# A depthwise convolution on TensorE, and sixteen output blocks under way during the modulation

## The chip, the cores and the metric

One core of one Trainium2 chip runs the whole kernel as one launch. The metric is the device time of that launch in microseconds. An execution of this kernel on the same chip repeats to some tenths of a per cent; three runs of the kernel before are given below.

The engines are named as the profile names them: PE is TensorE's matmul stream and PEld its weight loads, DVE is VectorE, ACT is ScalarE, POOL is GpSimd, SP is SyncE, whose queue issues all the DMAs here. PSUM is the memory that matmuls write, in eight banks of 128 x 512 float32; the rest is in SBUF or in HBM.

## The reference

The program is a two-layer decoder trunk on 256 tokens of 2048 channels, all float32. Layer 0 mixes tokens by a causal convolution module, layer 1 by stick-breaking attention; each is followed by a gated feed-forward part. Only the beginning, layer 0's mixer, is touched by the change:

```python
shift, scale, gate = ada_ln(c, mix_mod_w[0], mix_mod_b[0])      # silu(c) @ (2048 x 6144), + bias, in three parts
h = rms_norm(x, mix_norm_g[0]) * (1.0 + scale) + shift
u = h @ pw1_w + pw1_b                                           # 2048 x 4096, the "first product"
val, gt = jnp.split(u, 2, axis=-1)
u = val * jax.nn.sigmoid(gt)
u = causal_depthwise_conv(u, dw_w, dw_b)                        # 31 taps for each channel
u = jax.nn.silu(layer_norm(u, ln_g, ln_b))
x = x + gate * (u @ pw2_w + pw2_b)                              # 2048 x 2048, the "second product"
```

After it come layer 0's feed-forward part (whose shift and scale come from `ffn0`, a second modulation of the same shape), layer 1 and a last norm.

## The kernel before

Activations lie transposed, channels on the 128 partitions and the 256 tokens along the row: `xs[k]`, 16 tiles. A product keeps 128 x 128 blocks of weights in the array and moves 256 tokens past them. Weights come in **pieces** of eight blocks (512 KB, `raw`). Each piece is split into a high and a low part, `wh` by ScalarE (L213) and `wl` by VectorE (L214), and activations are split likewise (`hh`, `hl`; `zh`, `zl` for the second product). A block is then three matmuls (L251 `hh x wh`, L252 `hl x wh`, L253 `hh x wl`) into the block's PSUM bank.

**The modulation.** 128 columns of a modulation are one load of 1 MB (`mraw`) and one VectorE instruction that multiplies it by silu(c) and sums along the row (L276, `mod_reduce`); a small addition (L280) and, for the scale, L286 follow. Some parts go to TensorE instead: `mod_rows` multiplies silu(c) with 512 columns at a time, as float32 matmuls with 32 columns of weights in four column tiles of the array at once (L466), and turns the rows into columns with four small matmuls (L476) after ScalarE has copied the sums out of PSUM (L471). Before, the gate of `mix0`, the scale of `ffn0` and a part of the shift of `ffn0` are summed by TensorE.

**The head of the first product.** The contraction tiles of `h` become final one by one, as their scale and shift do (`start_tiles`): L276 twice, then `t` (L363, VectorE: x times scale times 1/rms), `hh` (L320) and `hl` (L321). Eight output blocks are under way at once, each in a bank of its own, so that each new tile has one piece of weights to meet. The other 24 blocks follow one after the other with all 16 tiles ready; the modulations to come run beside them as steps of a generator (`fill`, 0.6 steps a piece). Twelve of the later pieces are not split: they go to TensorE as float32 (L249, with `hf`, the sum of `hh` and `hl`, made by GpSimd, L506).

**The convolution.** When both halves of a channel tile are done, ScalarE takes the sigmoid (L524) and VectorE the product `u` (L528). `conv` then makes 31 taps of it: ScalarE multiplies 12 (L541), which GpSimd adds (L543, L545), VectorE does 18 as multiply-adds into a PSUM bank (L549), ScalarE the last one (L535), and L552 adds the two sums into `ys[j]`. It runs as a generator in `side`, beside the product.

**The layer norm and the second product.** Sums over channels are matmuls with a matrix of ones (L569), of 14 tiles first; from them comes a first mean, which VectorE subtracts (L580), ScalarE squares (L582) and TensorE sums (L583). Then come the deviation (L349, L351), two VectorE instructions and a Silu per tile (L622, L623, L624), the split (L317, L318), and the second product.

**What sets the order.** Each engine works through its instructions in a fixed order. The framework places them when the program is built, by priorities and by its own estimate of when each can run; semaphores make an engine wait. All loads stand in SP's queue in the order of the program (`load`), so a DMA that waits holds back those behind it. `raw` has six buffers, `mraw` three, the split weights four.

Of the kernel before, what the change touches and what calls it, by code (L numbers as in the profile page):

```python
# [17 lines left out]
PB = 8  # 128x128 blocks of weights in a piece  # L18
# [7 lines left out]
PRODUCTS = 8       # buffers between ScalarE and GpSimd  # L26
# [10 lines left out]
def plan(nbs, kts, first, stagger=4):  # L37
    """Order of the (output block, contraction tile) pairs of a product."""
# [9 lines left out]
class Cfg:  # L48
    def __init__(self, D, T, H, F, CW, FW):
# [3 lines left out]
        self.GH = 4  # L53
        self.rows0 = min(ROWS, KD // 4 - 1)

# [15 lines left out]
        items = [("c", KD), ("mix_g0", KD), ("mix_b0", 3 * KD), ("pw1_b", 2 * KD), ("cdw", KD * CW), ("cdb", KD), ("ln_g", KD), ("ln_b", KD),  # L71
# [6 lines left out]
        pl["pw1"] = plan(pairs, kd, min(8, 2 * KD), 0)  # L78
# [29 lines left out]
def hybrid_trunk(ctx: ExitStack, tc: tile.TileContext, cfg: Cfg, io: dict):  # L108
# [28 lines left out]
    # ---------------------------------------------------------------- constants and activations  # L137
# [53 lines left out]
    plain = {("pw1", i) for i in range(KD, 4 * KD) if i % PLAIN[0] == PLAIN[1]} if KD > 8 else set()  # L191
# [13 lines left out]
    def split_next():  # L205
        """High and low parts, of 12 significant bits each, of the next piece of weights."""
        blocks, v, n = raws[len(parts)]
        if stream[len(parts)] in plain:
            parts.append((blocks, v, None))
            return  # L210
# [6 lines left out]
    def pieces(name):  # L217
        """The pieces of a plan; loads and splits run ahead, over the ends of the plans."""
# [15 lines left out]
    def gemm(name, xh, xl, done, after=None, banks=(), x=None, width=None):  # L234
        """Weights stationary: psum[128 outputs, T] for each output block; done(block, psum)."""
        set_rate(name)
        left, ps, banks = {}, {}, list(banks)
        for nb, _ in cfg.plans[name]:
            left[nb] = left.get(nb, 0) + 1
        for blocks, wh, wl in pieces(name):  # L240
            for b, (nb, kt) in enumerate(blocks):
                first = nb not in ps
                if first:
                    ps[nb] = (banks.pop(0) if banks else psum_acc)()
# [3 lines left out]
                if wl is None:  # L248
                    nc.tensor.matmul(o, wh[:, c], x[kt], start=first, stop=left[nb] == 0)  # L249
                else:  # L250
                    nc.tensor.matmul(o, wh[:, c], xh[kt], start=first, stop=False)  # L251
                    nc.tensor.matmul(o, wh[:, c], xl[kt], start=False, stop=False)  # L252
                    nc.tensor.matmul(o, wl[:, c], xh[kt], start=False, stop=left[nb] == 0)  # L253
# [113 lines left out]
    class Entry:  # L367
# [585 lines left out]
```

## Time and profile before

| | us |
|---|---|
| three runs | 2379.94, 2383.69 (median), 2388.55 |
| span of the profiled execution | 2373.7 |
| median less that span | 10.0 |
| mean granted TensorE clock | 0.983 |
| sixteenth modulated tile `hh` starts | 134.8 |
| last matmul of the first product (L249) ends | 323.8 |
| first Silu of the layer norm (L624) | 356.5 |
| first matmul of the second product (L251 with `zh`) | 357.9 |

The profiled execution has no time of its own beside its span; the span runs from the first to the last instruction on the core. A row of the groups gives the line, engine, operation, output and input tiles, their shapes, the count, and then the busy time, the mean of one in ns and what the engine waited for just before. A row of the chain or of the timeline gives the start, the length, the engine, the tile and the line. In rows by stretch, a busy engine is followed by the number of its records in brackets.

### The profile page before, as it was taken

What the parts mean: (1) busy time and instruction counts of PE and PEld (TensorE: products, weight loads), DVE (VectorE), ACT (ScalarE), POOL (GpSimd) and SP (SyncE); (2) the same over time, 40 slices, a digit from 0 to 9 for tenths busy, and PEclk for the clock granted to TensorE, in tenths of its full rate; (3) what the DMA queues carried; (4) which work ended last, traced back from release to release, by engine and by line L of the source; (5) the groups of instructions that cost most, each with busy time, mean ns of one, the idle gap of its engine ahead of it and who ended that gap; (6) DMA issues with size and microseconds to landing.
All of it is one profiled execution on the core that took longest, in us unless ns stands there. A gap on an engine that the chain in (4) does not pass through costs nothing.

```text
span 2373.7 us, 45095 instructions
## 1 busy us (share of the span) xinstructions
PE 2280.7 (96%) x18228; PEld 2194.9 (92%) x18228; DVE 1814.1 (76%) x2470; ACT 1219.0 (51%) x1828; POOL 335.1 (14%) x357
## 2 busy tenths in 40 slices
PE   5689989999999999999999999999999999999997
PEld 4677859999999999999998999999999999999997
DVE  8978988898878788788887667789876555666644
ACT  3266667665553345555465544556555434555443
POOL 2368652300000000000121000121000000000011
PEclk8799999999999999999999999999999999999999
DMA  8987879677769877778866676676865555566663
GB/s 341 350 342 279 299 261 354 209 264 282 274 249 354 311 275 291 265 278 322 317 239 241 240 254 238 239 250 260 292 216 187 187 187 187 187 188 187 188 186 105
DMA packets 138308, 603.62 MB, mean 254 GB/s; under 512 B 15346, under 2 KB 15474, under 8 KB 113522
## 3 DMA queue, kind: packets, MB, share of 16 engines
q1 hardware_dynamic: 138098, 600.74, 71.5%
q8 instruction: 142, 2.33, 0.4%
q14 instruction: 68, 0.55, 0.1%
HBM read 598.58 MB, written 2.10 MB: 253 GB/s over the span
## 4 chain that ended last, share of the span: by engine, by line
PE 82%; DVE 10%; issue 2%; POOL 2%; DMA 2%; ACT 2%; DVEq 0%; SPq 0%; POOLq 0%; ACTq 0%
PE ps L252 25%; PE ps L251 25%; PE ps L253 25%; DVE mraw L276 3%; DVE wl L214 2%; POOL y L545 2%; DMA mraw<-in_mt_ffn 1%; PE ps L787 1%; PE ps L788 1%; PE ps L789 1%; PE ps L249 1%; DVE auxb L549 1%; PE auxa L466 1%; DVE t L363 0%; DVE hl L321 0%
## 5 line engine op out<-in xcount | busy, mean ns | idle before, releaser
L213 ACT CAST wh<-raw 128x1024 fp32r<-128x1024 f32 x740 | 773.8, 1048 | 884.9 <-PE ps L252 652.1
L214 DVE TENSOR_TENSOR wl<-raw,wh 128x1024 fp32r<-128x1024 f32 x740 | 910.2, 1234 | 379.0 <-ACT wh L213 372.0
L251 PE MATMUL ps<-hh,wh 128*128 128x256 f32 (+1 forms) x3696 | 1036.6, 284 | 49.2 <-ACT hh L320 48.1
L252 PE MATMUL ps<-hl,wh 128*128 128x256 f32 (+1 forms) x3696 | 1044.1, 283 | 4.0 <-DVE hl L318 2.0
L253 PE MATMUL ps<-hh,wl 128*128 128x256 f32 (+1 forms) x3696 | 1039.0, 281 | 6.3 <-DVE wl L214 6.3
L251 PEld LDWEIGHTS ps<-hh,wh 128*128 128x128 f32 x3696 | 694.2, 190 | 63.0 <-ACT hh L320 52.5
L252 PEld LDWEIGHTS ps<-hl,wh 128*128 128x128 f32 x3696 | 709.2, 192 | 9.3 <-issue 3.4
L253 PEld LDWEIGHTS ps<-hh,wl 128*128 128x128 f32 x3696 | 704.2, 191 | 11.5 <-DVE wl L214 7.3
L252 PE MATMUL ps<-gl,wh 128*128 128x256 f32 x1408 | 396.2, 281 | 0.0
L251 PE MATMUL ps<-gh,wh 128*128 128x256 f32 x1408 | 396.2, 281 | 0.0
L253 PE MATMUL ps<-gh,wl 128*128 128x256 f32 x1408 | 396.2, 281 | 0.0
L276 DVE CUSTOM_DVE_ANT_0 mraw<-mraw,csr 128x2048 f32<-128x2048 f32 x152 | 347.6, 2287 | 56.2 <-DMA mraw<-in_mt_ffn 34.8
L336 POOL TENSOR_TENSOR sumsq<-sumsq,t 128x256 f32<-128x256 f32 x56 | 70.2, 1254 | 1570.4 <-ACT t L332 1570.1
L252 PEld LDWEIGHTS ps<-gl,wh 128*128 128x128 f32 x1408 | 265.0, 188 | 0.0
L251 PEld LDWEIGHTS ps<-gh,wh 128*128 128x128 f32 x1408 | 265.0, 188 | 0.0
L253 PEld LDWEIGHTS ps<-gh,wl 128*128 128x128 f32 x1408 | 265.0, 188 | 0.0
L656 DVE SCALAR_TENSOR_TENSOR t<-ps,par,t 128x254 f32<-128x254 f32 x336 | 160.4, 479 | 4.1
L545 POOL TENSOR_TENSOR y<-y,prod 128x256 f32<-128x256 f32 x160 | 144.4, 911 | 12.9 <-ACT prod L541 3.0
L549 DVE SCALAR_TENSOR_TENSOR auxb<-u,cpar,auxb 128x256 f32<-128x256 f32 x288 | 118.8, 481 | 1.1 <-ACT auxb L535 0.9
L541 ACT ACTIVATE prod<-u,cpar 128x256 f32<-128x256 f32 x192 | 85.5, 500 | 40.3 <-DVE u L528 24.1
L653 ACT ACTIVATE t<-ps,par 128x256 f32<-128x256 f32 x168 | 93.9, 560 | 0.0
L332 ACT ACTIVATE t<-x 128x256 f32<-128x256 f32 x75 | 30.1, 414 | 85.9 <-DVE x L676 37.0
(174 smaller groups left out, 2107.9 us busy)
## 6 DMA issues: line engine op xcount, KB each, us to landing
raw<-in_w_down SPq DMA_DIRECT2D x176, 512.0 KB, 4.3
mraw<-in_mt_mix SPq DMA_DIRECT2D x80, 1024.0 KB, 7.3
mraw<-in_mt_ffn SPq DMA_DIRECT2D x72, 1024.0 KB, 6.7
raw<-in_w_pw SPq DMA_DIRECT2D x96, 512.0 KB, 6.2
raw<-in_w_up01b SPq DMA_DIRECT2D x84, 512.0 KB, 4.9
raw<-in_w_up11b SPq DMA_DIRECT2D x84, 512.0 KB, 3.5
raw<-in_w_up00b SPq DMA_DIRECT2D x80, 512.0 KB, 4.6
raw<-in_w_up10b SPq DMA_DIRECT2D x80, 512.0 KB, 3.6
```

Of the source, the lines that this page charges most:

```text
L213: nc.scalar.copy(wh[:, :n], v[:, :n])
L214: nc.vector.tensor_tensor(wl[:, :n], v[:, :n], wh[:, :n].bitcast(F32), op=ALU.subtract)
L251: nc.tensor.matmul(o, wh[:, c], xh[kt], start=first, stop=False)
L252: nc.tensor.matmul(o, wh[:, c], xl[kt], start=False, stop=False)
L253: nc.tensor.matmul(o, wl[:, c], xh[kt], start=False, stop=left[nb] == 0)
L276: nc.vector.tensor_tensor_reduce(out=v, in0=v, in1=csr, scale=1.0, scalar=0.0, op0=ALU.mult, op1=ALU.add, accum_out=macc[:, nb:nb + 1])
L336: engine.tensor_tensor(self.sum, self.sum, sq, op=ALU.add)
L541: nc.scalar.activation(pr, u[:, i:i + T], AF.Copy, scale=tap(i))
L545: nc.gpsimd.tensor_tensor(y, y, pr, op=ALU.add)
L549: nc.vector.scalar_tensor_tensor(o, u[:, k:k + T], tap(k), o, op0=ALU.mult, op1=ALU.add)
L653: nc.scalar.activation(y, ps[:, :T], AF.Identity, bias=pc(f"fdb{i}", nb, 1), scale=w(FW - 1))
L656: nc.vector.scalar_tensor_tensor(y[:, s:], ps[:, :T - s], w(k), y[:, s:], op0=ALU.mult, op1=ALU.add)
```

## The change

The convolution moves to TensorE. A channel tile of 128 is read as four blocks of 32 channels. For each block, `u` is written four times into `wide`, on the four quarters of the partitions, each copy one token further: a matmul then contracts 4 taps x 32 channels at once, and eight of them, four tokens apart, make 32 taps (the last is zero). Their weights are 128 x 32 matrices with the taps of four steps on diagonals, which GpSimd builds (`taps`, L559). The four blocks of 32 channels go to four column tiles of the array. So a tile is 32 float32 matmuls with 256 moving columns (L568) and one ScalarE instruction that adds the bias (L573); for each group of two tiles SP issues 16 copies from SBUF to SBUF, 64 KB each. ScalarE's, GpSimd's and VectorE's taps are gone.

The first product has 16 blocks under way in the head, two to a bank (value and gate of a channel tile), and so two pieces for each new tile (`gemm_pairs`). All pieces are split; L249 and `hf` are gone. `t` is made by ScalarE from `ys`, x / rms, which GpSimd writes ahead. The gate of `mix0` and the scale of `ffn0` are summed by VectorE (`mod_part`), not by TensorE. The steps beside the product go from 0.6 and 0.7 a piece to 1.06 and 1.25. The buffer that the launch sets aside for another kind of DMA is made smaller.

```diff
-POOL_TAPS = 12     # conv taps that ScalarE multiplies and GpSimd adds; VectorE has the others
-CONV_PACE = 0.7    # steps of the running convolutions after each piece
-PLAIN = (4, 3)     # of each 4 pieces of pw1, the one that goes to TensorE as float32, unsplit
+HEAD = 16
+SH = 4
+CONV_PACE = 1.25
-PW1_RATE, BUBBLE, LN_STEPS = 0.6, 8, 7
+PW1_RATE, BUBBLE, LN_STEPS = 1.06, 8, 7
...
-        pl["pw1"] = plan(pairs, kd, min(8, 2 * KD), 0)
+        pl["pw1"] = plan(pairs, kd, min(HEAD, 2 * KD), 0)
...
+    def gemm_pairs(name, xh, xl, done, after, banks):
+        ps, left = {}, {}
+        for i, (blocks, wh, wl) in enumerate(pieces(name)):
+            for b, (nb, kt) in enumerate(blocks):
+                j = nb % KD
+                first = j not in ps
+                if first:
+                    ps[j], left[j] = (banks.pop(0) if banks else psum_acc)(), 2 * KD
+                left[j] -= 1
+                o = ps[j][:, nb // KD * T:(nb // KD + 1) * T]
+                c = slice(b * P, (b + 1) * P)
+                mm = [(wh, xh), (wh, xl), (wl, xh)]
+                for k, (w, x) in enumerate(mm):
+                    nc.tensor.matmul(o, w[:, c], x[kt], start=first and k == 0, stop=left[j] == 0 and k == 2,
+                                     skip_group_check=True)
...
         def mods0():
-            yield from mod_rows("mix0", 2 * KD // 4, KD // 4)
+            yield from mod_part("mix0", 2)
...
-            yield from mod_rows("ffn0", KD // 4, KD // 4)
+            yield from mod_part("ffn0", 1)
...
+        for kt in range(KD):
+            nc.gpsimd.tensor_tensor(ys[kt], xs[kt], rs, op=ALU.mult)
...
-                hh[kt], hl[kt] = modulate_tile("mix0", kt, rs)
-                nc.gpsimd.tensor_tensor(hf[kt], hh[kt].bitcast(F32), hl[kt].bitcast(F32), op=ALU.add)
+                nc.scalar.activation(t, ys[kt], AF.Identity, bias=modv["mix0"][:, kt:kt + 1],
+                                     scale=moda["mix0"][:, kt:kt + 1])
+                split_act(t, hh[kt], hl[kt])
...
-                    pr = cpool2.tile([P, T], F32, name="prod", bufs=PRODUCTS)
-                    nc.scalar.activation(pr, u[:, i:i + T], AF.Copy, scale=tap(i))
...
-                        nc.gpsimd.tensor_tensor(y, y, pr, op=ALU.add)
...
-                    nc.vector.scalar_tensor_tensor(o, u[:, k:k + T], tap(k), o, op0=ALU.mult, op1=ALU.add)
...
+            for s in range(SH):
+                for i in range(SH):
+                    load(u[i * C32:(i + 1) * C32, :n, :], v[s * C32:(s + 1) * C32, i, :n, PADW - s:PADW - s + T])
+            for j in g:
+                t = cpool2.tile([P, SH * NM, C32], F32, name="taps", bufs=3)
+                nc.gpsimd.tensor_tensor(t, w.unsqueeze(2).to_broadcast([P, SH * NM, C32]),
+                                        pc("eye").unsqueeze(1).to_broadcast([P, SH * NM, C32]), op=ALU.mult)
...
+            for a, j in enumerate(g):
+                o = psum_b()[:, :T]
+                for m in range(NM):
+                    for i in range(SH):
+                        nc.tensor.matmul(o[i * C32:(i + 1) * C32, :], taps[a][:, i * NM + m, :],
+                                         v[:, i, a, SH * m:SH * m + T], start=m == 0, stop=m == NM - 1,
+                                         tile_position=(0, i * C32))
...
+                nc.scalar.activation(ys[j], o, AF.Identity, bias=pc("cdb", j, 1))
```

How the change moves instructions is seen at two places, in the fixed orders of the engines. The **first** is SP's queue where the head ends, before the change (`par` and `cst` are two small loads of constants; the `raw` behind them are the pieces after the head):

```order
L195 DMA par<-in_params 128x912
L195 DMA cst<-in_consts 128x144
L195 DMA raw<-in_w_pw 128x1024 x5
L195 DMA mraw<-in_mr_mix 128x2048
L195 DMA raw<-in_w_pw 128x1024 x2
```

And with the change, from the same two loads on:

```order
L194 DMA par<-in_params 128x912
L194 DMA cst<-in_consts 128x144
L194 DMA wide_218<-u 32x2x256 x16
L194 DMA wide_219<-u 32x2x256 x16
L194 DMA mraw<-in_mt_mix 128x2048
L194 DMA raw<-in_w_pw 128x1024 x5
```

The 32 copies of the first two groups of tiles, each of which needs the products `u` of its group, now stand ahead of the next pieces. TensorE's queue at the same place with the change (L268 is a matmul of the head, `auxb` a bank that the convolution writes, and the last row begins the product's second half):

```order
L268 MATMUL auxb<-hl_1376,wh 128x256
L268 MATMUL auxb<-hh_1375,wl 128x256
L568 MATMUL auxb<-wide_218,taps 32x256 x32
L568 MATMUL auxb<-wide_219,taps 32x256 x2
L568 MATMUL auxb<-wide_218,taps 32x256
L568 MATMUL auxb<-wide_219,taps 32x256
L568 MATMUL auxb<-wide_218,taps 32x256 x4
L568 MATMUL auxb<-wide_219,taps 32x256 x29
L568 MATMUL auxb<-wide_218,taps 32x256 x11
L568 MATMUL auxb<-wide_219,taps 32x256 x5
L268 MATMUL ps<-hh_236,wh 128x256
```

So 85 convolution matmuls stand ahead of the second half's first product.

The **second** place is the start of the second product, TensorE's queue before (`zh` and `zl` are its split inputs, `t` with `ones_d` the last sum of the layer norm, `hot` is silu(c)):

```order
L583 MATMUL ps<-t,ones_d 128x256
L466 MATMUL auxa<-mraw,hot 32x512 x11
L251 MATMUL ps<-zh_3521,wh 128x256 x4
L252 MATMUL ps<-zl_3522,wh 128x256
L253 MATMUL ps<-zh_3521,wl 128x256
```

And with the change, where L481 and L491 are what L466 and L476 were, and L244 and L245 what L251 and L252 were:

```order
L605 MATMUL ps<-t,ones_d 128x256
L481 MATMUL auxa<-mraw,hot 32x512 x24
L491 MATMUL ps<-cst,mraw 128x2 x4
L244 MATMUL ps<-zh_3474,wh 128x256
L245 MATMUL ps<-zl_3475,wh 128x256
```

The four small matmuls L491 now stand ahead of the whole product. They read `mraw`, which ScalarE writes at L486. That engine's queue with the change (L648 is Silu, L332 the split; `zh_3578` is the fourteenth of 16 tiles):

```order
L648 ACTIVATE t<-t,cpar 128x256
L332 CAST zh_3578<-t 128x256
L486 COPY mraw<-auxa 128x512
L360 ACT_TABLE_LOAD
L648 ACT_TABLE_LOAD
L648 ACTIVATE t<-t,cpar 128x256 x2
```

The copy stands behind fourteen Silus and splits.

More of the change, by code (lines that the diff above doesn't have):

```diff
@@ L53, in __init__ @@
         self.GH = 4
+        self.NM = -(-CW // SH)
         self.rows0 = min(ROWS, KD // 4 - 1)
@@ L232, in set_rate, with gemm @@
                 pace["rate"], pace["credit"] = rate
-    def gemm(name, xh, xl, done, after=None, banks=(), x=None, width=None):
+    def gemm(name, xh, xl, done, after=None, width=None):
         set_rate(name)
-        left, ps, banks = {}, {}, list(banks)
+        left, ps = {}, {}
         for nb, _ in cfg.plans[name]:
@@ L247, in gemm @@
                 c = slice(b * P, (b + 1) * P)
[L248 to L253, printed above, removed]
+                nc.tensor.matmul(o, wh[:, c], xh[kt], start=first, stop=False)
+                nc.tensor.matmul(o, wh[:, c], xl[kt], start=False, stop=False)
+                nc.tensor.matmul(o, wl[:, c], xh[kt], start=False, stop=left[nb] == 0)
                 if left[nb] == 0:
@@ L494, in hybrid_trunk @@
         hh, hl = [None] * KD, [None] * KD
-        hf = [cpool2.tile([P, T], F32, name=f"hf{k}") for k in range(KD)]
         ready = {"k": 0}
+        ys = [cpool.tile([P, T], F32, name=f"y{j}") for j in range(KD)]
+        for kt in range(KD):
+            nc.gpsimd.tensor_tensor(ys[kt], xs[kt], rs, op=ALU.mult)
         def start_tiles(n):
@@ L507, in start_tiles @@
             ready["k"] = min(KD, ready["k"] + n)
[L509 to L511 removed]
+        PADW, C32, NM = CW - 1, P // SH, cfg.NM
         st, nfill = {}, [0]
[L513 to L529 removed]
@@ new lines, in hybrid_trunk, with pw1_done @@
+        group_of = {j: g for g in groups for j in g}
+        wide = [cpool2.tile([P, SH, 2, PADW + T], F32, name=f"wide{i}") for i in range(2)]
+        for v in wide:
+            nc.gpsimd.memset(v[:, :, :, :PADW], 0.0)
+            nc.gpsimd.memset(v[:, :, :, PADW + T - SH + 1:], 0.0)
+        u_of = {}
+        def pw1_done(j, ps):
+            g = group_of[j]
+            if j == g[0]:
+                u_of[j] = cpool2.tile([P, 2, T], F32, name="u", bufs=5)
+            u = u_of[g[0]][:, j - g[0], :]
+            sg = t256()
+            nc.scalar.activation(sg, ps[:, T:2 * T], AF.Sigmoid, bias=pc("pw1_b", j + KD, 1))
+            nc.vector.scalar_tensor_tensor(u, ps[:, :T], pc("pw1_b", j, 1), sg, op0=ALU.add, op1=ALU.mult)
+            if j == g[-1]:
+                side.append(conv(g, u_of.pop(g[0])))
```

95 lines of the change are left out of this document (35 added, 60 removed).

## The prediction

> **What bounds the kernel now.** I read the page first (busy shares, TensorE's 40 slices, the chain), then the busy time by stretches, then the chain of waits in order of time where TensorE is not full.
>
> ```profile
> PE 2280.7 (96%) x18228; PEld 2194.9 (92%) x18228; DVE 1814.1 (76%) x2470; ACT 1219.0 (51%) x1828; POOL 335.1 (14%) x357
> PE   5689989999999999999999999999999999999997
> PE 82%; DVE 10%; issue 2%; POOL 2%; DMA 2%; ACT 2%; DVEq 0%; SPq 0%; POOLq 0%; ACTq 0%
> ```
>
> TensorE carries 82% of the chain; only the first slices (59 us each) have room. The change touches nothing after the second product, where VectorE's program is the same row for row, so only the first 460 us count.
>
> ```profile
> 60.00:80.00 20.00, 13.66 (x69) 13.25 (x70) 19.62 (x28) 3.50 (x6) 8.15 (x3) 0.68 0.92 346
> 120.00:140.00 20.00, 13.84 (x74) 13.11 (x75) 16.99 (x24) 6.03 (x9) 6.16 (x3) 0.74 1.00 383
> 380.00:400.00 20.00, 20.00 (x173) 20.00 (x172) 16.36 (x22) 13.83 (x29) 7.08 (x4) 1.00 0.93 348
> 400.00:420.00 20.00, 20.00 (x172) 20.00 (x171) 20.00 (x28) 10.38 (x18) 6.44 (x3) 1.00 1.00 397
> ```
>
> Columns: stretch, then busy us of PE, PEld, DVE, ACT, POOL, the clock, the DMA share, GB/s. At 380 TensorE is full: 173 matmuls in 20 us, 0.1156 us each, 2.78 us for a piece (24). During the modulation (60) VectorE is busy 19.6 of 20 and DMA 0.92; TensorE does 69 matmuls at clock 0.68. One contraction tile there, in the chain (start, us, what):
>
> ```profile
> 23.66 0.48 DVE hl L321
> ...
> 38.83 2.21 DVE mraw L276
> 41.08 0.59 DVE v_mix L280
> 41.88 0.49 DVE t L363
> 42.37 2.20 DVE mraw L276
> 44.72 1.23 DVE wl L214
> 45.95 0.40 DVE hl L321
> 46.34 2.20 DVE mraw L276
> ...
> 134.83 0.52 ACT hh L320
> ```
>
> A step is 7.51 us, all VectorE; the sixteenth modulated tile is out at 135.
>
> **The head (16 blocks).** VectorE's step loses `t` (0.49, now GpSimd and ScalarE) and gains the split of a second piece (1.23): 8.25 us. DMA per step: two modulation tiles of 1.05 MB and two pieces of 0.52 MB, 3.15 MB; at 383 to 397 GB/s 7.9 to 8.2 us, at 346 9.1. I take 8.4, nearest to VectorE's bound, since the queue at share 1.00 just keeps up; ends 8.25 and 9.1. The first tile waits once for GpSimd's multiply:
>
> ```profile
> L506 POOL TENSOR_TENSOR hf<-hh,hl 128x256 f32<-128x256 f32 x16 | 41.5, 2592 | 94.6 <-DVE hl L321 94.6
> 61.00:62.00 1.00, 1.00 (x7) 1.00 (x6) 1.00 (x2) 0.00 (x0) 0.58 (x1) 0.50 1.27 381
> 71.00:72.00 1.00, 1.00 (x11) 1.00 (x9) 0.90 (x5) 0.39 (x1) 0.64 (x1) 1.00 0.94 389
> ```
>
> 2.59 for 0.49 is +2.1, the other fifteen run ahead. Last tile: 134.83 + 15 x 0.9 + 2.1 = 150.4; 48 matmuls after it (5.6) end the head at 156.5. TensorE's 48 matmuls are 5.6 us at full clock; at the pace of the stretch at 60, 13.66 / 69 = 0.20 each, they are 9.6 and exceed the step. The two rows of single microseconds show the clock at 0.50 and then full, and with hardly a gap left between the bursts I expect it full and add nothing; if it stayed, the head would be 16 x 1.2 = 19 us longer. The Trainium skill (TensorE: Matmul & The Clock Gate, Part 1) says that about 3.4 us of sustained work frees the clock: by it a step's matmuls end after some 7 us and the sum stands, by the pace at 60 it would be 19 us more; the row at 71 agrees with the rule.
>
> **From the head to the last matmul of the product.** These are the prices:
>
> ```profile
> 185.83 0.81 SPq L195 DMA_DIRECT2D raw<-in_w_pw  x2
> out<-x SPq DMA_DIRECT2D x8, 256.0 KB, 2.0
> 320.15 3.61 PE L249 MATMUL ps<-hf,raw 128*128 128x256 f32 x16
> 219.28 1.06 PE L466 MATMUL auxa<-mraw,hot 128*32 128x512 f32 x8
> 258.01 0.95 PE L476 MATMUL ps<-cst,mraw 128*128 128x4 f32 x8
> 325.55 1.99 PE L569 MATMUL ps<-y,ones_d 128*128 128x256 f32 x8
> ```
>
> An issue on SP takes 0.405 us, a small transfer lands 2.0 us after it. No weights for the second half are asked for before 32 small copies (order, first place): ready about 3 us before the head ends, they are issued from 153.4 to 166.4; the first sixteen are there at 161.9, the others at 168.4. TensorE waits, does one tile's convolution, waits, does 37 more of its matmuls (4.7); ScalarE's two evacuations stand ahead of the first split, so the product resumes near 175, 18.5 us on, with 93 convolution matmuls done.
>
> A convolution matmul is float32 with 32 columns of weights, four side by side. Four of the same kind with 512 moving columns take 1.06 (8 records, L466); half of that is 0.53 for 256 columns. One float32 pair at full width takes 3.61 / 8 = 0.45: no less. L476, eight records bound by loading weights, takes 0.95: no more. I take 0.50, between the two nearest. Then to the last matmul of the product: 32 pieces x 2.78 = 89.0; 355 convolution matmuls / 4 x 0.50 = 44.4; 14 sums (L569, 0.49) 6.9; 5 for small waits, about what it loses now. 175 + 145.3 = 320.3. Now L249 ends at 323.8, so **-3.5**. In this sit the removed work: 12 pieces at 3.61 become 2.78 (-10.0), and 26 of L466's 40 groups (-28). What leaves the other engines is covered by TensorE and earns nothing:
>
> ```profile
> L549 DVE SCALAR_TENSOR_TENSOR auxb<-u,cpar,auxb 128x256 f32<-128x256 f32 x288 | 118.8, 481 | 1.1 <-ACT auxb L535 0.9
> L276 DVE CUSTOM_DVE_ANT_0 mraw<-mraw,csr 128x2048 f32<-128x2048 f32 x152 | 347.6, 2287 | 56.2 <-DMA mraw<-in_mt_ffn 34.8
> ```
>
> VectorE gives up 119 us and takes 32 reductions (73) and 12 splits (15); per piece it then has 2.29 + 1.23 = 3.5 us against TensorE's 145 / 32 = 4.5, so it keeps up. GpSimd builds 16 tap matrices of 1024 columns, not seen before: at most 4 x 2.59 = 10.4 us each by L506, two for each group of 8 pieces (36 us), three ahead in the head; covered, and 10 us a group if that cover goes.
>
> **The tail and the second product.**
>
> ```profile
> 329.38 7.80 DVE y L580 x14
> 337.17 7.12 DVE auxb L549 x19
> ...
> 349.57 0.44 DVE y L580
> ...
> 356.46 0.65 ACT t L624 x2
> ...
> 378.87 0.59 ACT L471 COPY mraw<-auxa 128x512 f32<-128x512 f32 x1 [0.68 <-PE auxa L466]
> 461.40 0.43 PE auxb L340 x2
> ...
> L624 ACT ACTIVATE t<-t,cpar 128x256 f32<-128x256 f32 x16 | 9.0, 595 | 2.1 <-DVE t L623 2.0
> L317 ACT CAST zh<-t 128x256 fp32r<-128x256 f32 x16 | 5.8, 397 | 0.1
> ```
>
> From the last matmul to the first Silu (L624) it is 32.7 us now. After the change the last `u` stands in VectorE's queue behind seven subtractions, two reductions and two splits, so about 6 us late; 16 issues (6.5), landing (2.0), its convolution behind the previous tile's (to about 23), the last subtraction behind two more reductions (25.4); from that subtraction to Silu stays 6.9 (349.57 to 356.46): 32.3. I count **0**; ends -10 and +8.
>
> The second product started 1.4 us after the first Silu. Now TensorE's queue has the four small matmuls of the shift columns (L491) ahead of it, and they need ScalarE's copy of `auxa`, which stands behind 14 of the 16 tiles `zh` (order, second place). Silu 0.595 and cast 0.397 for 14 tiles are 13.9, the copy 0.59, L491 (as L476) 0.95: 15.4, so **+14.0**. What waits behind it is the whole product. Nothing of L466 and L476 is left inside that product: 4 x 1.06 + 0.95 = **-5.2**.
>
> **Sum**: -3.5 + 0 + 14.0 - 5.2 = +5.3 on a span of 2373.7: 2379.0. The median shown lies 10.0 above that span, so **2389**.
>
> **Rivals.** *Faster, through the tail* (2376): the last tile's convolution now costs VectorE 7.1 us behind 7.8 of subtractions; if `u` goes to its copies at once, 0.9 + 6.5 + 2.0 + 4.0 + 1.0 + 6.9 = 21 replaces 32.7, -11, and a convolution group at 0.47 takes 2.7 more: 2389 - 13. It decides once the tail is under 26 us. Against it: VectorE's order, and TensorE at half clock in sparse work.
>
> *Slower, the loads* (2409): in the second half 32 pieces, 28 modulation tiles and 80 copies are 51.4 MB; at 346 GB/s 149 us, and while SP issues a group's copies it moves 1 MB in 6.5 us where 3.0 would do, 5 x 3.5 = 17 more. From 166.4 that is 332, and 5 to split and multiply: 337, +17 on my 320.3; with a step of 8.6 in the head, +3. For it: share 0.92 gave 346. Against it: 397. The Trainium skill (DMA: Bandwidth & Descriptors, Specifications) gives about 358 GB/s from HBM per core; by that the step would be 8.8 and the time 2395 before the copies; the rows at 383 and 397 differ from it, so the measurement decides against the rule.
>
> *Slower, the array* (2433): if 32-column weights load as L476's do, 0.95 a group: 89 x 0.45 + 4 = +44. Against it: L466's eight records in 1.06 with twice the columns.
>
> *The 16 blocks do not come free*: the clock stays at half in the head, +19, 2408; counted with the loads.
>
> **How the numbers follow.** A measurement here tells no change from 0.3%, 7.2 us. My forecast has 0.45 (its own range 2378 to 2398: 0.33 within 0.3%, 0.11 slower, 0.01 faster), the tail 0.27 (0.25 faster, 0.02 within), the loads or the half clock 0.20 (0.19 slower, 0.01 within), the array 0.08. Faster 0.26, within 0.36, slower 0.38. The range of 2366 to 2412 takes in the tail's end and the loads, and leaves the array out.
>
> **What would show it.** Right: hh steps of 8.3 to 8.5 us; TensorE idle or on L568 for about 18 us after the head; groups of eight L568 records each 0.5 us; the last L268 of the first product near 320; L491 waiting for ScalarE's copy until some 14 us after the first Silu; the same length after that. Wrong: TensorE waiting for wh or wl by DMA again and again between 175 and 320 (the loads), L568 at 0.9 (the array), a tail under 26 us, or a second product that starts with the first `zh`.

## The result, and the profile after

| | before | after |
|---|---|---|
| median | 2383.82 | 2435.51 (2434.70 to 2442.46) |
| span of the profiled execution | 2373.7 | 2434.5 |
| sixteenth `hh` starts | 134.8 | 156.9 |
| product goes on after the head | 139.9 | 191.6 |
| last matmul of the first product ends | 323.8 | 362.1 |
| first Silu of the layer norm | 356.5 | 403.5 |
| first matmul of the second product | 357.9 | 418.6 |
| last matmul of the second product starts | 455.4 | 514.2 |

After by before is 1.0234, 95% interval 1.0209 to 1.0259: slower by 2.3%, and the prediction of 2389 (2366 to 2412) was wrong. All of it is lost before the second product begins: 60.7 us there, 60.8 at the end of the span. The medians lie only 51.7 us apart. In every other execution on record the span is 1.7 to 2.0 us below the time; if that holds for the profiled execution of the kernel before too, it was some 8 us faster than the median, and most of the 10.0 between the two is scatter.

Of the page of the changed kernel, these are the busy shares, TensorE and its clock in 40 slices of 61 us, and the chain by engine:

```profile
PE 2302.5 (95%) x19076; PEld 2219.7 (91%) x19076; DVE 1785.6 (73%) x2226; ACT 1161.5 (48%) x1664; POOL 196.0 (8%) x196
PE   5869886999999999999999999999999999999997
PEclk9989997999999999999999999999999999999999
PE 79%; DVE 9%; DMA 4%; issue 3%; ACT 2%; SPq 2%; POOL 0%; DVEq 0%; ACTq 0%; POOLq 0%
```

Slices 3 to 7 of TensorE, at 8, 9, 9, 8 and 9 tenths before, are at 6, 9, 8, 8 and 6, and two shares of the chain have grown: DMA from 2 to 4% and SP's queue from 0 to 2%. By stretches (columns as in the prediction):

```profile
60.00:80.00 20.00, 15.40 (x113) 14.95 (x113) 18.67 (x25) 6.57 (x9) 0.00 (x0) 0.91 0.98 367
160.00:180.00 20.00, 9.34 (x92) 7.16 (x90) 3.38 (x7) 3.32 (x7) 1.91 (x1) 0.83 0.41 92
220.00:240.00 20.00, 18.03 (x243) 13.73 (x245) 2.41 (x2) 1.42 (x3) 3.82 (x2) 1.00 0.60 182
240.00:260.00 20.00, 17.72 (x179) 16.05 (x171) 20.00 (x16) 6.46 (x8) 6.21 (x2) 1.00 0.86 312
380.00:400.00 20.00, 10.38 (x88) 4.80 (x92) 6.11 (x11) 4.00 (x6) 0.00 (x0) 0.70 0.62 231
```

The head (60) is as forecast: 113 matmul records in 20 us for 69, at a granted clock of 0.91, the DMA share 0.98. At 160 the DMA engines move 92 GB/s and TensorE is busy 9.3 of 20; at 220 VectorE is busy 2.4 of 20, waiting for loads that were asked for late. SP's queue shows why, from the head's end on (start, length until the last issue of the row, what):

```profile
160.57 20.61 SPq L194 DMA_DIRECT2D wide<-u  x32
181.22 0.58 SPq L194 DMA_DIRECT2D mraw<-in_mt_mix  x1
181.91 2.56 SPq L194 DMA_DIRECT2D raw<-in_w_pw  x5
...
203.48 29.07 SPq L194 DMA_DIRECT2D wide<-u  x32
...
247.95 14.70 SPq L194 DMA_DIRECT2D wide<-u  x16
```

The 32 copies take 20.61 us, 0.64 each, not 13.0. The next 32 take 29.07, 8.6 more than 32 such issues. Their `u` was there by 164.3; what SP waits for between them is the landing of earlier loads. These are SP's longest waits for DMAs, and its wait for `u`, in the whole run (us in all, times, longest):

```profile
SPq L194 <- DMA raw<-in_w_pw: 17.5, 15, 2.7
SPq L194 <- DMA mraw<-in_mt_ffn: 15.7, 9, 2.8
SPq L194 <- DVE u L545: 13.5, 1, 13.5
```

`u` is waited for once, at the head's end. The waits for DMAs follow an order that the trace shows: a DMA of SP is issued only after the one eight places ahead of it in the queue has landed. At the 959 places where both times are recorded there is no exception, and the two always share a semaphore. So the copies just behind a row of loads wait for these loads: 23 copies, after waits of 32 us in all, were issued within 0.1 us of such a landing.

The weights behind the copies are asked for afterwards, and the chain of waits goes through them (the last two rows are a load and a copy that waits for it to land):

```profile
181.91 6.91 DMA raw<-in_w_pw
188.84 1.05 ACT wh L209
189.91 1.66 DVE wl L210
191.62 5.67 PE ps L268 x46
...
247.47 9.46 DMA raw<-in_w_pw
256.94 0.58 SPq L194
```

### The profile page after: what moved, and what is told of

Its sections match the earlier page's. It is cut to its first block, busy times and chain, and to the rows that moved or that the text cites. A ratio compares the mean times of both kernels' runs of the same rounds, so it can differ in the third digit from the quotient of the medians.

```text
span 2434.5 us, 46382 instructions
## 1 busy us (share of the span) xinstructions
PE 2302.5 (95%) x19076; PEld 2219.7 (91%) x19076; DVE 1785.6 (73%) x2226; ACT 1161.5 (48%) x1664; POOL 196.0 (8%) x196
## 4 chain that ended last, share of the span: by engine, by line
PE 79%; DVE 9%; DMA 4%; issue 3%; ACT 2%; SPq 2%; POOL 0%; DVEq 0%; ACTq 0%; POOLq 0%
PE ps L245 24%; PE ps L244 24%; PE ps L246 24%; DVE mraw L291 3%; SPq L194 2%; DVE wl L210 2%; DMA raw<-in_w_pw 2%; PE ps L268 1%; PE ps L811 1%; PE ps L812 1%; PE ps L813 1%; DMA mraw<-in_mt_mix 1%; ACT wh L209 1%; DMA mraw<-in_mt_ffn 1%; DVE hl L333 0%
## 5 line engine op out<-in xcount | busy, mean ns | idle before, releaser
L209 ACT CAST wh<-raw 128x1024 fp32r<-128x1024 f32 x752 | 787.8, 1049 | 933.3 <-PE ps L245 649.9
L210 DVE TENSOR_TENSOR wl<-raw,wh 128x1024 fp32r<-128x1024 f32 x752 | 925.6, 1235 | 371.6 <-ACT wh L209 365.1
L245 PE MATMUL ps<-hl,wh 128*128 128x256 f32 (+1 forms) x3328 | 930.8, 280 | 3.6 <-DVE hl L333 2.1
L244 PE MATMUL ps<-hh,wh 128*128 128x256 f32 (+1 forms) x3328 | 933.8, 281 | 0.0
L246 PE MATMUL ps<-hh,wl 128*128 128x256 f32 (+1 forms) x3328 | 927.1, 279 | 4.6 <-DVE wl L210 4.6
L245 PEld LDWEIGHTS ps<-hl,wh 128*128 128x128 f32 x3328 | 630.3, 189 | 4.4 <-DVE hl L333 2.5
L244 PEld LDWEIGHTS ps<-hh,wh 128*128 128x128 f32 x3328 | 625.2, 188 | 0.4
L291 DVE CUSTOM_DVE_ANT_0 mraw<-mraw,csr 128x2048 f32<-128x2048 f32 x184 | 430.2, 2338 | 146.9 <-DMA mraw<-in_mt_mix 85.9
L245 PE MATMUL ps<-gl,wh 128*128 128x256 f32 x1408 | 396.2, 281 | 0.0
L244 PE MATMUL ps<-gh,wh 128*128 128x256 f32 x1408 | 396.2, 281 | 0.0
L245 PEld LDWEIGHTS ps<-gl,wh 128*128 128x128 f32 x1408 | 265.0, 188 | 0.0
L244 PEld LDWEIGHTS ps<-gh,wh 128*128 128x128 f32 x1408 | 265.0, 188 | 0.0
L268 PE MATMUL ps<-hh,wh 128*128 128x256 f32 x416 | 116.8, 301 | 38.5 <-ACT hh L332 33.9
L268 PE MATMUL ps<-hh,wl 128*128 128x256 f32 x416 | 123.2, 299 | 16.0 <-DVE wl L210 16.0
L268 PE MATMUL ps<-hl,wh 128*128 128x256 f32 x416 | 122.5, 298 | 1.3 <-DVE hl L333 1.3
L268 PEld LDWEIGHTS ps<-hh,wh 128*128 128x128 f32 x416 | 79.2, 199 | 45.1 <-ACT hh L332 37.8
L268 PEld LDWEIGHTS ps<-hh,wl 128*128 128x128 f32 x416 | 84.8, 204 | 21.0 <-DVE wl L210 21.0
```

The costliest lines, as they stand in the source:

```text
L209: nc.scalar.copy(wh[:, :n], v[:, :n])
L210: nc.vector.tensor_tensor(wl[:, :n], v[:, :n], wh[:, :n].bitcast(F32), op=ALU.subtract)
L268: nc.tensor.matmul(o, w[:, c], x[kt], start=first and k == 0, stop=left[j] == 0 and k == 2, skip_group_check=True)
L291: nc.vector.tensor_tensor_reduce(out=v, in0=v, in1=csr, scale=1.0, scalar=0.0, op0=ALU.mult, op1=ALU.add, accum_out=macc[:, nb:nb + 1])
```

## The experiments

Times are of one execution each, unless a ratio stands with them; the kernel before took 2383.6 to 2386.5 beside them on the same chip, and 2379.55 (a median of 17) in experiments 9 to 11. Four executions of the changed kernel lie between 2434.7 and 2442.5, so the time alone does not tell a difference under about 7 us. Places in the program are read from the profile of each and are steadier: the sixteenth `hh` starts between 156.8 and 157.2 in all the kernels below that do not touch it.

**1. The copies on GpSimd's queue**

```diff
-                    load(u[i * C32:(i + 1) * C32, :n, :], v[s * C32:(s + 1) * C32, i, :n, ...])
+                    tc.keep_in_program_order(nc.gpsimd.dma_start(v[s * C32:(s + 1) * C32, i, :n, ...], u[...]))
```

> Edit: the 144 copies of the convolution are issued by GpSimd's own DMA queue, not by SP's; nothing else moves. Theory Q (SP's queue): a group's 16 copies, 0.64 us each on SP, and the wait of the first for u, hold back the weights and modulation tiles that stand behind them, so with the copies gone from SP the pieces after the head are there when the head ends (the product resumes some 20 us earlier than 191.6) and the second half loses its waits for raw: about 2395. Rival B (bandwidth): the second half is limited by the bytes that it moves, which stay the same, so 2430 to 2440. Rival A (array): the convolution's matmuls limit it, so 2430 to 2440 too.

Measured: 2431.8. The copies no longer hold back SP, and nothing is gained that the time can tell. In the uses of the tile `wide`, the row of the issues and the last row show what took their place:

```profile
L554 POOL DMA_DIRECT2D wide<-u x144: 496/533/710, 162.5 to 388.2; - x144
DMA to landing us min/median/max: 1.7/7.2/9.4
```

A copy now lands 7.2 us (median) after its issue; on SP's queue that was 2.0. The loads fill the DMA engines (share 1.03 at 160, 1.02 at 200) and a copy gets its turn among them. GpSimd's queue too issues eight copies and then waits for landings:

```profile
162.47 4.41 POOL L554 DMA_DIRECT2D wide<-u  x8 [112.47 <-DVE u L545]
168.91 0.53 POOL L554 DMA_DIRECT2D wide<-u  x1 [2.03 <-DMA wide<-u]
```

The first 32 take 30.2 us there instead of 20.6. By share the DMA engines are busy 186 of the 200 us from 160 to 360, against 157 in the changed kernel: now they are nearly full. TensorE's fixed order has the convolution ahead of the product, so it waits for `wide` instead of weights: the first product ends at 374.5, 12 us later than in the changed kernel; the tail to the first Silu is 31.4 us, 10 shorter, and the second product begins 1.4 us after that Silu. So B's time came out, though not for the bytes alone; A gave the same time, and experiment 3 decides about it. The Trainium skill (DMA: Bandwidth & Descriptors, Issuing engines are not separate DMA queues) says that DMAs issued by different engines run on the same 16 DMA engines and interleave; the 7.2 beside the 2.0 agrees.

**2. A quarter of the copies**

```diff
-            nc.gpsimd.memset(v[:, :, :, :PADW], 0.0)
-            nc.gpsimd.memset(v[:, :, :, PADW + T - SH + 1:], 0.0)
+            nc.gpsimd.memset(v, 0.0)
...
-            for s in range(SH):
+            for s in range(1):
```

> Edit: only 4 of each group's 16 copies are made, for the first quarter of the partitions (the other three quarters of wide stay zero, so 3 of 4 taps are left out of the result); all matmuls stay. Theory Q: 108 issues of 0.64 us less on SP, 15 us at the end of the head and 7.7 for each of the seven later groups, of which some 5 are in the way: 2385 to 2395. Rival B: 7 MB less of 51, 18 us at 383 GB/s: 2417. Rival A: no change, 2435.

Measured: 2391.5, 44 less; the first product ends at 330.6 instead of 362.1 and TensorE is busy 20.0 of 20 from 180 to 280. That is theory Q's range. The bytes do not account for it, neither with the 18 us of rival B nor with 28, which 6.3 MB take at the 224 GB/s reckoned below for copies; nor does the array, for which nothing would have changed.

**3. A quarter of the convolution's matmuls**

```diff
-                for m in range(NM):
+                for m in (0, NM - 1):
...
-                    if m == NM // 2 - 1:
+                    if m == 0:
```

> Edit: of a tile's 32 convolution matmuls only 8 are made (the first and the last step of four taps; the other 24 taps are left out of the result); all copies stay. Theory Q and rival B: TensorE waits for weights anyway, so at most 5 us less in the second half, and 2 in the tail: 2428 to 2435. Rival A: 3/4 of 89 groups of four at 0.46 us fall away, 30 us: 2405.

Measured: 2429.1. Three quarters of the convolution on TensorE are worth 6.4 us, within what theory Q and rival B allow and far from the 30 of rival A: the array isn't the bound.

**4. Eight blocks in the head**

```diff
-HEAD = 16
+HEAD = 8
```

> Edit: 8 blocks under way in the head instead of 16, everything else as changed. The head's step falls to VectorE's 7.0 to 7.5 us, its end from 163 to about 148; 16 pieces more remain for after it, which is 44 us of matmuls at 2.78 each. If 16 blocks are a gain even so (theory: the head hides two pieces for each step), this is slower than the changed kernel by 15 to 30: 2450 to 2465. If the second half is limited by the 32 modulation tiles and the copies, which are the same, the extra pieces fill its gaps and it comes out within 10 us: 2430 to 2445.

Measured: 2456.1; the first product ends at 396.5, 34 us later. Beside this convolution the 16 blocks are a gain of 20 us at the end.

**5. The copies as ScalarE instructions**

```diff
-                    load(u[i * C32:(i + 1) * C32, :n, :], v[s * C32:(s + 1) * C32, i, :n, ...])
+                    nc.scalar.copy(v[s * C32:(s + 1) * C32, i, :n, ...], u[i * C32:(i + 1) * C32, :n, :])
```

> Edit: the 16 copies of a group are instructions of ScalarE (32 partitions of u to another 32 of wide), no DMA; nothing else moves. What the first runs left: on GpSimd's queue the copies no longer held back the loads, but each landed 7.2 us after its issue in place of 2.0 and TensorE waited for wide, so two theories stand. Theory Q2 (the copies cost the DMA rings their time, wherever they are issued): without them the second half moves 46 MB, 123 us at 376 GB/s, less than TensorE's 145, and TensorE becomes the bound: product ends some 30 us earlier than 362, tail 9 shorter, 2390 to 2400. Rival C (ScalarE becomes the bound instead): 16 copies at 0.59 (as its 128 x 512 copy) are 9.4 us a group ahead of the splits that the product needs next; some 3 to 5 us lost for each of eight groups: 2415 to 2425. Rival D (what limits is TensorE's fixed order, product behind convolution): 2430.

Measured: 2403.8, 32 less, between Q2 and C. The first product ends at 345.8, 16 earlier; the tail is 32.2 us instead of 41.4. From 160 on TensorE is nearly full, but for two places where the chain runs through ScalarE's copies (165 to 173 and 197 to 218); the first of them:

```profile
165.28 0.49 ACT wide L554
165.78 0.62 ACT wide L554
...
172.71 0.63 ACT wide L554
173.47 0.59 PE auxb L568 x2
```

So as DMAs the copies cost at least the 32. As ScalarE instructions, 0.62 each for 32 x 512, they still cost something: TensorE stands idle 4.9 us from 160 to 180 and 2.4 from 200 to 220, about what C said for a group, but at two of eight places.

**6. Loads ahead of the first copies**

```diff
                     start_tiles(1)
+                    if ready["k"] == KD:
+                        look["load"], look["split"] = 5, 3
```

> Edit: the loads and splits run 5 and 3 pieces ahead from the last step of the head on, so four pieces stand ahead of the first 32 copies in SP's queue (and 160 of the product's matmuls ahead of the convolution in TensorE's). Theory Q: the product goes on at once when the head ends, and the 28 us from the head's end at 163 to 191.6 are worked through; some of it is lost again to the later groups, whose copies still hold back the loads: 2410 to 2420. Rival B (bytes): four pieces earlier are worth their 2.1 MB, 6 us: 2427 to 2431.

Measured: 2438.5; both misses. The step itself does what was meant, TensorE is full right after the head, yet the product ends at 359.8, 2.3 us earlier:

```profile
160.00:180.00 20.00, 20.00 (x193) 17.86 (x192) 7.13 (x12) 6.40 (x12) 0.00 (x0) 0.96 0.36 80
180.00:200.00 20.00, 16.61 (x227) 11.79 (x222) 9.82 (x6) 4.88 (x7) 11.81 (x4) 1.00 0.86 325
```

While TensorE works at 160 the DMA engines again move only copies (80 GB/s). The work that TensorE does earlier it waits for later. That fits a half that is limited by the stream through SP's queue: there it does not matter when TensorE starts.

**7. The steps before the second product**

```diff
-PW1_RATE, BUBBLE, LN_STEPS = 1.06, 8, 7
+PW1_RATE, BUBBLE, LN_STEPS = 1.06, 8, 0
```

> Edit: no step of the modulation to come is forced between the two layer-norm parts (LN_STEPS 7 to 0), so the four small matmuls L491 and the ScalarE copy that they wait for come after the second product has begun. Prediction's step: the second product begins 15.2 us after the first Silu because L491 stands ahead of it; without it 1.4 us after, and nothing of this is given back: 13 to 14 less, 2421 to 2422. Rival: the product is then held by the Silus, one tile in 1.0 us, and takes the remaining groups of L481 (1.06 each, 2 of 8) and L491 back inside: 8 less, 2427.

Measured: 2428.4. The second product begins at 405.5, 1.4 us after the first Silu (404.1), 13.1 earlier than with the change. It then takes 100.3 instead of 95.6 to its last matmul, so 8.4 are left there, and the time is 7.1 less: the rival was right. The wait was not all loss; part of what it held up was done in it.

**8. `t` by VectorE**

```diff
-            nc.gpsimd.tensor_tensor(ys[kt], xs[kt], rs, op=ALU.mult)
...
-                nc.scalar.activation(t, ys[kt], AF.Identity, bias=..., scale=...)
-                split_act(t, hh[kt], hl[kt])
+                hh[kt], hl[kt] = modulate_tile("mix0", kt, rs)
```

> Edit: t is made by VectorE again (one instruction from x, scale and 1/rms), GpSimd's 16 multiplies are gone. Theory P: in the first steps VectorE's small instructions took 0.57 instead of 0.17 and its reduction 2.7 instead of 2.2 while GpSimd multiplied (22 to 50 us), and that made the sixteenth hh late; without it these steps return to 8.3, 5 to 6 us earlier, and the 0.49 for t is hidden by the wait for ScalarE that the step has (t, hh, wh, wl one after the other): hh16 at 151, time 2428 to 2430. Rival: the 0.49 comes back on VectorE in all 16 steps, 8 us: hh16 at 158, time 2435 to 2438.

Measured: 2430.8. The sixteenth `hh` starts at 150.1 instead of 156.9, as theory P had it; the time, 4.7 less, is 0.8 above its range.

**9. The copies through HBM**

```diff
...
-            for s in range(SH):
-                for i in range(SH):
-                    load(u[i * C32:(i + 1) * C32, :n, :], v[s * C32:(s + 1) * C32, i, :n, ...])
+            d = dpool.tile([2, SH, C32, T], F32, name="ud")
+            load(u[:, :n, :], d[:n].rearrange("n i c t -> (i c) n t"))
+            for s in range(SH):
+                load(d[:n].rearrange("n i c t -> c (n i) t"), v[s * C32:(s + 1) * C32, :n, ...])
...
```

> Edit: a group's copies go through HBM: one DMA writes u there, four read it back into wide (wide's inner order changed to suit), so 5 issues on SP in place of 16 and a quarter more bytes moved in pieces of 1 KB. Theory Q (SP's time and its in-order hold is the larger part): 11 issues of 0.64 less for each group, some 50 us of SP in the second half, and less than 10 us of DMA time more: 2400 to 2415. Rival E (the DMA time of the copies' small packets is what counts, 42 us of all 16 engines for 9.4 MB by the stretch from 160 to 180, where 92 GB/s took a share of 0.41): 25% more of it, 10 us slower: 2440 to 2450.

Measured: 2408.4, 27 less with a quarter more bytes (23 less if each is taken against the kernel before on its own chip). The first product ends at 339.7, 22 earlier. By share the DMA engines are busy 163 of the 180 us from 160 to 340, in the changed kernel 157 of the 200 from 160 to 360: they have no less to do, they only stand idle less. So about half of the loss is SP's issues and waits, not the DMA time of the small packets. The other half this run does not divide, since the shape of the copies changed with their number. (The 9.4 MB in the expectation should be 8.4: 112 copies of 64 KB and 32 of 32 KB.)

**10 and 11. The single edits together**

```diff
-                    load(u[i * C32:(i + 1) * C32, :n, :], v[s * C32:(s + 1) * C32, i, :n, ...])
+                    (nc.scalar.copy if (s + i) % 2 else nc.vector.tensor_copy)(v[...], u[...])
```

with the edits of 6, 7 and 8; in the second kernel half of the copies go to ScalarE and a quarter each to VectorE and GpSimd.

> Edit: the copies are instructions, half on ScalarE and half on VectorE; loads and splits run ahead from the last head step; t by VectorE; no forced modulation steps before the second product (the edits of copies_act, loads_first, t_vector and shift_later together). By the terms found singly: copies off the DMA rings -33, half of ScalarE's 27 us of waits in the second half gone -13, t by VectorE -5, the early loads worth the wait at the head's end now that nothing holds the stream -8, the forced steps -6 to -10: 2435 - 65 to -69 = 2366 to 2370. If VectorE, 14 of 20 us busy there, becomes the bound by the 72 copies (some 25 us more): 2385. If the gain of the head is eaten by the convolution's 58 us on TensorE however well the rest is hidden, it ends at 2380 to 2390, level with the kernel before.

> Edit: as all_moved_2, but a quarter of the copies each on VectorE and GpSimd and half on ScalarE. If VectorE limits all_moved_2, this is 5 to 10 us faster; if GpSimd's own pace (its 128 x 256 multiply took 1.75 us, with VectorE slowed meanwhile) makes the last copy of a group late, 5 to 10 us slower.

Measured: 2373.45, ratio to the kernel before 0.9971 (0.9954 to 0.9988), and 2374.95, ratio 0.9974 (0.9964 to 0.9984). Both are a little faster than the kernel before, by 0.3%, and about 61 us faster than the changed one; the first lies 3 to 7 us above the 2366 to 2370 that I reckoned. VectorE is now nearly full beside TensorE:

```profile
200.00:220.00 20.00, 20.00 (x252) 15.28 (x256) 20.00 (x16) 5.03 (x7) 6.50 (x3) 0.97 0.96 367
240.00:260.00 20.00, 18.17 (x184) 16.09 (x182) 19.80 (x23) 9.07 (x13) 3.04 (x2) 1.00 0.94 351
by line: PE ps L268 28.9%; PE auxb L562 23.6%; PE ps L244 5.9%; PE ps L245 5.6%; PE ps L246 5.5%; DVE wide L548 4.1%; DVE mraw L291 3.9%; PE ps L599 3.2%; DVE wl L210 3.2%; issue 3.1%; PE ps L585 2.5%; ACT wide L548 2.5%; PE auxa L481 2.3%;
```

That is all_moved_2, two stretches and its chain from 150 to 400. VectorE is busy 20.0 and 19.8 of 20, where it had 14.6 and 20.0 after the change, but TensorE has some 77% of the chain and VectorE some 11%. With GpSimd taking a quarter of the copies nothing differs that can be told, so the second kernel does not show VectorE to be the bound. It relieved VectorE by little: the copies left to it took 0.72 us instead of 0.42 (medians), and its busy time from 140 to 360 fell only from 196 to 188. The first product ends at 322.8, 1.0 earlier than in the kernel before, and the second begins at 354.8, 3.1 earlier.

**12. The head's part alone**

```diff
-        pl["pw1"] = plan(pairs, kd, min(8, 2 * KD), 0)
+        pl["pw1"] = plan(pairs, kd, min(16, 2 * KD), 0)
...
-        gemm("pw1", hh, hl, pw1_done, x=hf, after=after_pw1, banks=[psum_acc] * 5 + [psum_a] + [psum_b] * 2)
+        gemm_pairs("pw1", hh, hl, pw1_done, after_pw1, [psum_acc] * 5 + [psum_a] + [psum_b] * 2, hf)
```

> Edit: the kernel before with one part of the change alone, 16 blocks under way in the head, two to a bank; the convolution stays on VectorE, GpSimd and ScalarE, the modulation parts stay on TensorE, t on VectorE (plain pieces remain among the last 32; three more buffers for u, room for them as in the change). Reckoning: the head's step is 7.51 + 1.23 for the second split, 8.7, so the sixteenth hh at 153 and the head's end near 159 instead of 140; after it VectorE has the work it had from 140 to 350 (187 us) without 12 splits (15): 172, so it is done at 325 to 331, and the first Silu comes at 340 to 348 instead of 356.5. Theory H (the head's part is the useful half of the change and the convolution's move is what loses): 2368 to 2376. Rival V (VectorE and GpSimd, 19 and 17 of 20 us busy there, are the bound whatever TensorE has done in the head): within 5 of the kernel before, 2379 to 2389.

Measured: 2408.6, 22 slower than the kernel before; V's mechanism, at a higher price than it gave. The first product ends at 317.2, 6.6 earlier than in the kernel before, but the first Silu comes at 384.7, 28 later. The old convolution cannot start before the head ends, and then GpSimd sets the pace:

```profile
180.00:200.00 20.00, 20.00 (x154) 15.87 (x152) 12.21 (x24) 15.14 (x29) 18.67 (x21) 1.00 0.83 330
220.00:240.00 20.00, 13.53 (x81) 10.08 (x81) 12.63 (x27) 15.31 (x31) 18.43 (x23) 0.74 0.32 124
```

18.4 to 18.7 of 20 on GpSimd (fifth pair), with TensorE short of work. The pace of the convolution's steps (0.7 a piece) was left as it was for 48 pieces, so some of it falls into the tail; how much a better pace would win was not tried. So, as built here, neither part by itself beats the kernel before (for the other one, together with the modulation's move to VectorE, experiment 4).

## Why the prediction was wrong

Each row is a step of the prediction, the place in the span that it gave and what was measured; the last column is what the step itself adds to the error.

| step | predicted | measured | adds |
|---|---|---|---|
| sixteenth `hh` | 150.4 | 156.9 | +6.5 |
| product goes on | 175 | 191.6 | +10.1 |
| first product ends | 320.3 | 362.1 | +25.2 |
| first Silu | 352.6 | 403.5 | +9.1 |
| second product begins | 368.0 | 418.6 | -0.3 |
| end of the span | 2379.0 | 2434.5 | +4.9 |

The sum, 55.5, is the error of the span; the forecast of 2389 missed the median by 46.5. The difference is the 8 or 9 us by which the profiled execution before was probably faster than its median.

**The step of the head** was right: 8.35 us (61.99 to 70.34 in the chain, from one first reduction to the next) for 8.4, and with the clock at 0.91 nothing of the 19 us for a half clock came. **The first tiles** were not. I let GpSimd's multiply cost 2.1 once and had the other fifteen "run ahead". They ran from 22 to 50 us, and VectorE was slower beside them. From the chain, a step in the second tile and one after GpSimd had finished:

```profile
29.98 2.74 DVE mraw L291
32.76 0.57 DVE v_mix L295
33.36 0.66 DVE a_mix L301
...
53.65 2.20 DVE mraw L291
55.89 0.17 DVE v_mix L295
```

The reduction takes 2.74 for 2.20, the small additions 0.57 and 0.66 for 0.17 and 0.16. In experiment 8, without the multiplies, the reduction at 28.51 takes 2.20 and the additions after it 0.17 each. That experiment gets 6.7 us back at the sixteenth `hh`, 4.7 of the time. The Trainium skill (SBUF — State Buffer, Who interferes with whom) says that a VectorE instruction with two SBUF inputs contends with a GpSimd instruction that reads SBUF; these rows agree, in which the reduction and the additions have two such inputs.

**The copies.** This is the step that failed: "An issue on SP takes 0.405 us", and with it the sum of the second half, in which TensorE works through with "5 for small waits" while the copies and what stands behind them in SP's queue cost nothing. The row was of a load from HBM; a copy within SBUF takes SP longer, and I gave its price no upper end although no row of before shows one:

```profile
L194 SPq DMA_DIRECT2D wide<-u x144: 507/594/1569, 160.6 to 387.6; - x144
```

A median of 594 ns, with the gap to the next 0.64 us: 20.6 instead of 13.0 at the head's end, 10.3 instead of 6.5 a group. That is 7.6 of the 10.1 in the table; the weights behind them, 6.9 us to land and 2.7 to split, are 1.8 more than the 8.6 I had from the last issue to the product. Experiments 2 and 5 show that the copies as DMAs are the cause, experiment 9 that about half of the loss is what SP has to issue and to wait for.

**The second half** took 170.5 us instead of 145.3, and TensorE stood idle 21 of the 160 us from 200 to 360. It belongs to the rival "Slower, the loads", whose mechanism was right: SP's queue, and one MB in the time of a group's copies. I gave it 0.20, and 17 us where 25 came (together with a later start). What it lacked is in the rows of the result. The copies hold the loads behind them not only for their issues but also while they wait themselves: of the 91.1 us that the five rows of copies between 203 and 365 take in SP's queue, 61.4 are 96 issues of 0.64, and nearly all of the other 29.6 are waits for earlier loads to land. (Experiment 1's expectation puts such waits down to `u`; the trace does so at the head's end only.) And a byte of a copy takes the DMA engines longer than one of a load. At 160 a share of 0.41 moved 92 GB/s, which is 224 at full share; loads alone, before the change, 376 (0.92 for 346). By this estimate the 8.4 MB of copies are 37 us of all DMA engines, and 46 MB of loads 123: 160 of the 201 us from the first copy to the end of the product. In the other 41 us the engines stood idle, and it is this idle time that experiment 9 shortened. The 397 GB/s that I held against the rival was a rate of loads without copies between them.

**The array** was priced well: the 32 convolution matmuls of a tile, 64 records, take 3.66 us (200.82 in TensorE's timeline), 0.457 for a group of four, where I took 0.50 between 0.45 and 0.95; its rival is out, by experiment 3 too.

**The tail** was counted at no change and got 9 us longer. The last `u` was there 2 us after the last matmul, sooner than I had it; its 16 copies were not. They stand behind seven loads, issued just before, and the second to the eighth copy each wait for one of these to land. SP's waits from 364 to 384 (in all, times, longest), and the chain:

```profile
SPq L194 <- DMA mraw<-in_mt_ffn: 5.6, 3, 2.7
SPq L194 <- DMA raw<-in_w_pw: 3.8, 4, 1.7
...
368.44 14.11 DMA raw<-in_w_pw
...
382.57 0.51 SPq L194
```

My 32.3 had 16 issues (6.5) and a landing (2.0) directly behind `u`. Without these DMAs the tail is 32.2 (experiment 5), with them on another queue 31.4 (experiment 1).

**The second product** began 15.1 us after the first Silu, 15.4 by the sum: the small matmuls behind ScalarE's copy were seen rightly, in the chain

```profile
416.11 0.58 ACT t L648
...
417.02 0.59 ACT mraw L486
417.65 1.05 PE ps L491 x8
```

But the price of that wait at the end is 7 to 8, not 14 (experiment 7). And of the -5.2 for work gone from inside the product only 1.9 is there (95.6 for 97.5), and 2.0 is lost again after it; where, the profiles do not show.

**The faster case** needed a tail under 26 us. In the changed kernel the copies, not VectorE's subtractions, were last; and without these DMAs the tail was still 32.2 (experiment 5) and 30.5 (experiment 10). With a quarter of them it was 25.9 (experiment 2); no run came to 21.

## What to carry to other kernels

A copy inside SBUF that is made by small DMAs was paid three times here: in the issuing queue (0.64 us each), in the DMA engines, and by every load that stands behind it in the same queue, above all while the copy itself waits for earlier loads to land; ask who stands ahead of it and behind it before moving work to an idle engine. While the stream of loads was the limit, giving the starved engine an earlier start was worth nothing (experiment 6). A price for an operation that the trace doesn't show needs an upper end, and the two halves of a change should be priced together: here each alone, as built, was slower than the kernel before, and with the copies made by ScalarE and VectorE and three smaller edits both together were 0.3% faster.

## What the hardware showed that I had not expected

- A DMA within SBUF, 32 partitions of 2 x 1 KB, took SP's queue 0.59 us to issue (median); a load of 128 partitions took it mostly 0.33 to 0.42.
- In SP's queue, and in GpSimd's in experiment 1, no DMA was issued before the one eight places ahead of it had landed. Each shares its semaphore with that one, so this may be the program's doing and not the chip's.
- Issued from GpSimd's queue beside a full stream of loads, the same copy landed after 7.2 us instead of 2.0 (medians).
- By share of busy time, an estimate, the copies would move 224 GB/s at full share, the loads 376.
- ScalarE moved 32 partitions of 512 elements to another 32 in 0.62 us (median, experiment 5), where its copy of 128 x 512 took 0.59; VectorE took 0.42 (median, experiment 10), at the longest 2.13.
- While GpSimd multiplied, VectorE's smallest additions took 0.57 us instead of 0.17.
